# Attention probabilities normalised and masked by GpSimd on copies made by ScalarE, gates in place, PSUM banks six and two

## The chip, the cores and the metric

The kernel runs on one core of one Trainium2 chip. The metric is the device time of one execution in microseconds (us); the time of before is the median of three runs. One further execution was recorded by the hardware profiler; the profile's numbers are of that one. Engines: TensorE (PE; its weight loads are PEld), VectorE (DVE), ScalarE (ACT), GpSimd (POOL), and SyncE (SP), which here only issues DMAs. SBUF is the core's memory of 128 partitions; PSUM is the memory that TensorE writes into, and its eight banks are each one tile of 128 x 512 fp32 here.

## What is computed

Two layers over 1024 tokens and 2048 features. Each layer normalises its input, multiplies it by `w_in`, sends pieces of the result through three heads side by side (sliding-window attention, a gated MLP over chunks, gated linear attention), gates their joint output with silu, and multiplies by `w_out`. Cut to what matters here:

```python
h = rms_norm(x, g_pre) * (1.0 + scale) + shift
a_q, a_k, a_v, s_u, s_v, c_q, c_k, c_v, c_g, z = split(h @ w_in)
# sliding-window attention: blocks of 128 queries, each sees its own block and the one before
scores = einsum('bnqgrd,bnkgd->bngrqk', qb, kb) * 64 ** -0.5
valid = (dist >= 0) & (dist < 128) & (not before the first token)
scores = where(valid, scores, -inf)
m = maximum(scores.max(-1), sink)
p = exp(scores - m)
probs = p / (p.sum(-1) + exp(sink - m))
y_a = einsum('bngrqk,bnkgd->bnqgrd', probs, vb)
y_b = chunked_spatial_gating(gelu(s_u), gelu(s_v), ...)
y_c = rms_norm(gated_linear_attention(c_q, c_k, c_v, log_sigmoid(c_g @ w_up + b) / 16))
out = (concat(y_a, y_b, y_c) * silu(z)) @ w_out
x = x + gate * rms_norm(out, g_post)
```

## The kernel before

**Phases.** Each layer runs over two halves of 512 tokens: four phases, each an `in_phase` (products with `w_in`) and an `out_phase` (products with `w_out`). An `in_phase` goes through groups of output columns; a group fills four PSUM banks from the pool `pj` and adds up over 16 tiles of features. Matrix products are fp32 made of three faster ones (high by high, high by low, low by high): `mm_f` (L382 to L384) for results laid out by feature, `mm_t` (L390 to L392) by token. Every piece of weights is split in high and low by a copy of ScalarE (L368) and a subtraction of VectorE (L369), into a pool of four buffers (`whl`).

**Lanes.** All other work hangs beside the groups: generators in lanes ("att", "gla", "sg", "mod", "fin"). After each three matmuls a group calls `tick()`, and a `yield n` in a lane passes n ticks, that is 3n matmuls of the group. So TensorE's order is a group's triples with the lanes' matmuls between. `drain` runs a lane to its end without ticks; at L810 it does so with the last unit of the first attention call of each phase. A scheduler orders each engine's instructions by priority, and `urgent()` raises it. All PSUM tiles outside the groups come from the pool `mx` (three banks before, `pj` five); who takes one waits until its use before is finished, and TensorE's queue behind it waits too.

**Attention.** There are 32 units, eight in each phase (a pair of heads by four blocks of queries). A unit's scores (L490) go into four `mx` tiles, two at a time; ScalarE copies the previous block's half (L499), VectorE the own block's under a mask (L500), into the tile M. Then come the row maximum, eight exponentials on ScalarE (L516), the sum and its reciprocal, and the product of M with the reciprocal on VectorE (L519, 128 x 1024 elements). After a lag come, for each of the two heads, four transposes on TensorE (L532) and the mask multiplication (L535): VectorE reads the transposed tile from PSUM twice and multiplies by `amask` (k <= q for the own block, k > q for the one before), 128 x 1024 elements into the tile PT. After a further lag the products with the values (L546) follow, which read PT, and a copy on ScalarE (L550). Units 3, 11, 19 and 27 (counted over the kernel) are those that L810 drains.

**Activations.** `silu2` writes tanh into a temporary of the pool t2 (four buffers) and VectorE makes the result from it. `gelu2` copies the bank into a temporary x (L436), squares it into a second, u (L437), and after four more steps the last (L441, on VectorE) reads u and x into the result.

**Gated linear attention (GLA).** `gates` transposes the gate columns (L569) from the tiles that the copy at L767 has brought out of PSUM. `gla_scores` makes its scores at several levels: matmuls `far` (L649) and `near` (L633) into two `mx` tiles, emptied by `put`, VectorE copies under a mask (L620; eight of 32 x 128 after each `near`).

**SyncE** issues all DMAs (weights, inputs, results); GpSimd clears tiles (L496, L598) and masks eight small weights once.

Of the kernel before, what the change touches and what calls it, by code (L numbers as in the profile page):

```python
# [10 lines left out]
F32 = mybir.dt.float32  # L11
# [4 lines left out]
AF = mybir.ActivationFunctionType  # L16
ALU = mybir.AluOpType
AX = mybir.AxisListType
PSUM = bass.MemoryType.PSUM
DRAM = bass.MemoryType.DRAM  # L20

P = 128
# [5 lines left out]
NT = H // P  # L28
# [11 lines left out]
def hybrid_kernel(ctx: ExitStack, tc: tile.TileContext, a, y_out):  # L40
    nc = tc.nc

    const = ctx.enter_context(tc.tile_pool(name="const", bufs=1))
# [5 lines left out]
    sm = ctx.enter_context(tc.tile_pool(name="sm", bufs=2))  # L49
    pj = ctx.enter_context(tc.tile_pool(name="pj", bufs=5, space=PSUM))  # L50
    mx = ctx.enter_context(tc.tile_pool(name="mx", bufs=3, space=PSUM))
    pools = {}

    V, S, G, PE = nc.vector, nc.scalar, nc.gpsimd, nc.tensor

    def load(out, in_):
        nc.sync.dma_start(out=out, in_=in_)
# [38 lines left out]
    def t2(shape=(P, 512), dt=F32):  # L96
        return t2_p.tile(list(shape), dt, tag="t2", name="t2")
# [7 lines left out]
    def mxt():  # L105
        return mx.tile([P, 512], F32, tag="mx", name="mx")

    def pjt():
        return pj.tile([P, 512], F32, tag="pj", name="pj")
# [7 lines left out]
    V.memset(ones, 1.0)  # L117
    amask = const.tile([P, 2, P], F32, name="amask")
    pmask = const.tile([P, P], U8, name="pmask")
# [305 lines left out]
    def silu2(dst, ps):  # L425

        t = t2()
        S.activation(t, ps, AF.Tanh, scale=0.5)
        V.scalar_tensor_tensor(dst, t, 1.0, ps, ALU.add, ALU.mult)

    def gelu2(dst, ps):

        x = t2()
        u = t2()
        with urgent():
            S.copy(x, ps)  # L436
        S.activation(u, x, AF.Square)  # L437
        V.tensor_scalar(u, u, 0.044715, 1.0, ALU.mult, ALU.add)
        V.tensor_tensor(u, u, x, ALU.mult)
        S.activation(u, u, AF.Tanh, scale=GELU_C)  # L440
        V.scalar_tensor_tensor(dst, u, 1.0, x, ALU.add, ALU.mult)  # L441

# [30 lines left out]
    def attention(l, h, g0, qt, vt, cst):  # L473
# [5 lines left out]
        for m in range(4):  # L479
# [3 lines left out]
            for bp in range(2):  # L483
                sps = [mxt().rearrange("p (b k) -> p b k", b=2) for _ in range(2)]
                for b in range(2):
                    n = 2 * bp + b
# [27 lines left out]
            den = col(8, "at_den")  # L514
# [3 lines left out]
            V.reciprocal(den, den)  # L518
            V.tensor_tensor(Mf, Mf, den.unsqueeze(2).broadcast_to([P, 8, P]), ALU.mult)  # L519
            if m < 3:  # L520
# [8 lines left out]
            for p in range(2):  # L529
                tp = mxt()  # L530
                for n in range(NT):
                    PE.transpose(tp[:, n * P:(n + 1) * P], M[:, p, n], ident)  # L532
                pt = pools["pt"].tile([P, 2, NT, P], F32, tag="PT", name="PT")
                with urgent():
                    V.tensor_tensor(pt, tp.rearrange("p (n q) -> p n q", n=NT).unsqueeze(1).broadcast_to([P, 2, NT, P]),  # L535
                                    amask.unsqueeze(2).broadcast_to([P, 2, NT, P]), ALU.mult)
                pts.append(pt)
                yield LAG["t"][p]
# [26 lines left out]

    def gates(l, cg):
        tp = mxt()
        for n in range(NT):
# [445 lines left out]
    with tc.tile_pool(name="start", bufs=1) as st:  # L1014
# [44 lines left out]
        rsqrt(r0, r0, H, st)  # L1059
        psk = [mxt()] + [pjt() for _ in range(5)]  # L1060

# [55 lines left out]
    load(gpc[1], a["g_pre"][1])  # L1117
    load(amask, a["k_amask"])
    pm32 = t2((P, P), I32)
# [33 lines left out]
    for k, (l, h) in enumerate(phases):  # L1153
# [22 lines left out]
        "w_out", "swa_sinks", "sg_w", "sg_b", "sg_ln_g", "sg_ln_b", "gla_w_gate_up", "gla_b_gate", "gla_norm_g",  # L1176
        "k_amask", "k_pmask", "k_gmask", "k_fcol"]


def layout(i):  # L1180
# [48 lines left out]
    k, q = np.meshgrid(r(P), r(P), indexing="ij")  # L1229
    o["k_amask"] = np.stack([k <= q, k > q], axis=1).astype(np.float32)  # L1230
    o["k_pmask"] = (q <= k).astype(np.int32)
# [31 lines left out]
```

## Time and profile before

| | |
|---|---|
| median of three runs | 3062.44 us (3062.06 to 3065.12) |
| the profiled execution | 3067.03 us, its span 3065.3 us |
| mean granted TensorE clock | 0.993 |
| busy: ScalarE, GpSimd | 1229.8 us (40%), 24.5 us (1%) |
| the normalising multiplication, L519 | 32 of 1223 ns |
| the mask multiplication, L535 | 64 of 1221 ns |
| the gelu's copy out of PSUM, L436 | 32 of 576 ns |

Of the profiled execution the page gives each engine's busy time and share, and the chain of work that ended last, followed back from the last instruction. Further views group TensorE's idle time by what ended it (a row says engine, tile and line, "<-", the releaser's engine, tile and line, then the total in us, how often, the longest), give busy times by windows, and list instructions by time. In a row of instructions a bracket at the end is the idle time before it and who ended it. "x8" at a row's end counts instructions that the row gathers.

### The profile page before, as it was taken

The numbers are of one execution on the slowest core, as the hardware profiler recorded it, in microseconds if no ns is written. First come the engines' busy times: TensorE is split into PE (matmuls) and PEld (weight loads), VectorE is DVE, ScalarE is ACT, GpSimd is POOL, SyncE is SP. The second block draws the span as 40 slices with busy tenths as digits, with TensorE's granted clock in tenths as the row PEclk, the third lists the DMA queues.
The fourth block names the chain that finished last, engine by engine and source line by source line (L and its number), as shares of the span: only waits on it lengthen the run. The fifth ranks groups of instructions, "written<-read, shape, count | busy, mean of one in ns | idle before, by whom it ended". The sixth has DMA issues, their size and how long they took to land.

```text
span 3065.3 us, 44211 instructions
## 1 busy us (share of the span) xinstructions
PE 3000.0 (98%) x17298; PEld 2440.8 (80%) x17298; DVE 1840.3 (60%) x2948; ACT 1229.8 (40%) x2415; POOL 24.5 (1%) x66
## 2 busy tenths in 40 slices
PE   8999999999998999999999999999999999999998
PEld 4678777888886888788888788888888888888886
DVE  4668778464767877644364766644346476663425
ACT  3355455232434544323243554423223455442322
POOL 0000000000000000000000000000000000000000
PEclk9999999999999999999999999999999999999999
DMA  9744457475784445544455223334446322343535
GB/s 394 276 138 152 141 179 224 131 243 158 223 255 154 129 138 184 164 126 141 123 159 163 83 73 100 121 114 144 120 124 192 106 83 83 114 133 105 165 103 162
DMA packets 214914, 468.98 MB, mean 153 GB/s; under 512 B 21008, under 2 KB 72624, under 8 KB 212656
## 3 DMA queue, kind: packets, MB, share of 16 engines
q1 hardware_dynamic: 214704, 466.15, 48.6%
q8 instruction: 136, 2.23, 0.3%
q14 instruction: 74, 0.61, 0.1%
HBM read 429.37 MB, written 36.70 MB: 152 GB/s over the span
## 4 chain that ended last, share of the span: by engine, by line
PE 81%; DVE 8%; DMA 6%; ACT 3%; issue 2%; SPq 0%; DVEq 0%; ACTq 0%
PE pj L382 12%; PE pj L390 12%; PE pj L392 12%; PE pj L383 12%; PE pj L384 12%; PE pj L391 12%; DMA wm<-in_w_mod_dram 3%; PE mx L490 2%; PE mx L546 2%; DVE whl L369 2%; DVE ma L225 1%; PE mx L532 1%; ACT whl L368 1%; PE mx L1076 1%; DMA t<-in_x_dram 1%
## 5 line engine op out<-in xcount | busy, mean ns | idle before, releaser
L369 DVE TENSOR_TENSOR whl<-wraw,whl 128x1024 fp32r<-128x1024 f32 (+2 forms) x504 | 587.3, 1166 | 720.9 <-ACT whl L368 719.9
L368 ACT CAST whl<-wraw 128x1024 fp32r<-128x1024 f32 (+2 forms) x504 | 505.0, 1002 | 1048.3 <-PE pj L392 494.6
L390 PE MATMUL pj<-whl,act 128*128 128x512 f32 (+1 forms) x2048 | 785.0, 383 | 0.5 <-ACT hold L767 0.5
L392 PE MATMUL pj<-whl,act 128*128 128x512 f32 (+1 forms) x2048 | 778.5, 380 | 0.0
L391 PE MATMUL pj<-whl,act 128*128 128x512 f32 (+1 forms) x2048 | 775.9, 379 | 0.0
L382 PE MATMUL pj<-act,whl 128*128 128x512 f32 x1904 | 756.4, 397 | 9.1 <-ACT t L436 8.2
L383 PE MATMUL pj<-act,whl 128*128 128x512 f32 x1904 | 744.2, 391 | 0.0
L384 PE MATMUL pj<-act,whl 128*128 128x512 f32 x1904 | 742.6, 390 | 0.0
L392 PEld LDWEIGHTS pj<-whl,act 128*128 128x128 f32 x2048 | 385.6, 188 | 72.2 <-issue 0.3
L390 PEld LDWEIGHTS pj<-whl,act 128*128 128x128 f32 x2048 | 386.3, 189 | 70.8 <-issue 2.5
L391 PEld LDWEIGHTS pj<-whl,act 128*128 128x128 f32 x2048 | 386.0, 188 | 67.0 <-issue 0.8
L382 PEld LDWEIGHTS pj<-act,whl 128*128 128x128 f32 x1904 | 358.5, 188 | 100.4 <-issue 14.3
L384 PEld LDWEIGHTS pj<-act,whl 128*128 128x128 f32 x1904 | 358.6, 188 | 76.5
L383 PEld LDWEIGHTS pj<-act,whl 128*128 128x128 f32 x1904 | 358.9, 188 | 70.7 <-issue 0.7
L225 DVE SCALAR_TENSOR_TENSOR ma<-wm,sc,ma 128x512 f32<-128x512 f32 x240 | 179.9, 750 | 61.6 <-DMA wm<-in_w_mod_dram 58.7
L516 ACT ACTIVATE M<-M,at_nm 128x128 f32<-128x128 f32 x256 | 99.6, 390 | 19.4 <-DVE at_nm L508 19.4
L535 DVE TENSOR_TENSOR PT<-mx,amask 128x1024 f32<-128x1024 f32 x64 | 77.8, 1221 | 17.1 <-PE mx L532 17.0
L500 DVE COPY_PREDICATED M<-pmask,mx 128x256 f32<-128x256 uint8 x128 | 51.2, 442 | 53.5 <-ACT M L499 41.5
L490 PE MATMUL mx<-kc,qs 128*128 128x256 f32 (+1 forms) x256 | 66.2, 288 | 10.5 <-DVE hold L620 5.9
L490 PE MATMUL mx<-kc,qlo 128*128 128x256 f32 (+1 forms) x256 | 65.8, 285 | 0.0
L499 ACT COPY M<-mx 128x256 f32<-128x256 f32 x96 | 31.7, 375 | 80.7 <-PE mx L490 80.7
L490 PEld LDWEIGHTS mx<-kc,qs 128*128 128x128 f32 x256 | 49.3, 193 | 17.7 <-issue 7.1
(230 smaller groups left out, 2390.1 us busy)
## 6 DMA issues: line engine op xcount, KB each, us to landing
wraw<-in_w_in_dram SPq DMA_DIRECT2D x312, 512.0 KB, 3.6
wraw<-in_w_out_dram SPq DMA_DIRECT2D x136, 512.0 KB, 3.6
wm<-in_w_mod_dram SPq DMA_DIRECT2D x256, 256.0 KB, 3.7
wm<-in_w_mod_dram SPq DMA_DIRECT2D x16, 2048.0 KB, 13.7
y<-at SPq DMA_DIRECT2D x64, 256.0 KB, 2.9
q<-y SPq DMA_DIRECT2D x64, 256.0 KB, 2.8
q<-x SPq DMA_DIRECT2D x36, 256.0 KB, 2.7
wraw<-in_w_vcg_dram SPq DMA_DIRECT2D x32, 272.0 KB, 2.8
```

The lines of the kernel that those rows point to most:

```text
L225: V.scalar_tensor_tensor(acc, ws[k], sc[:, k:k + 1], acc, ALU.mult, ALU.add)
L368: S.copy(hl[:, 0], raw)
L369: V.tensor_tensor(hl[:, 1], raw, hl[:, 0].bitcast(F32), ALU.subtract)
L382: PE.matmul(ps, lhsT=whi, rhs=slot[:, 0], start=(k == 0), stop=False)
L383: PE.matmul(ps, lhsT=whi, rhs=slot[:, 1], start=False, stop=False)
L384: PE.matmul(ps, lhsT=wlo, rhs=slot[:, 0], start=False, stop=(k == NK - 1))
L390: PE.matmul(ps, lhsT=slot[:, 0, c], rhs=whi, start=(k == 0), stop=False)
L391: PE.matmul(ps, lhsT=slot[:, 0, c], rhs=wlo, start=False, stop=False)
L392: PE.matmul(ps, lhsT=slot[:, 1, c], rhs=whi, start=False, stop=(k == NK - 1))
L490: PE.matmul(sps[p][:, b, k0:], lhsT=qi[:, p, n * P:(n + 1) * P], rhs=kc[2 * j + p][:, n * P + k0:n * P + 256], start=(part == 0), stop=(pa ...
L516: S.activation(Mf[:, k], Mf[:, k], AF.Exp, bias=nm[:, k:k + 1], scale=0.125, accum_out=den[:, k:k + 1])
L535: V.tensor_tensor(pt, tp.rearrange("p (n q) -> p n q", n=NT).unsqueeze(1).broadcast_to([P, 2, NT, P]), amask.unsqueeze(2).broadcast_to([P, ...
```

## The change

- The product of M with the reciprocals (L519) runs on GpSimd instead of VectorE.
- The mask multiplication (L535) is replaced: for each head two ScalarE copies of 128 x 512 from PSUM into PT's halves, then two GpSimd selects that put zero where the mask is zero. The constant `amask` and its load go.
- `silu2` and `gelu2` work in place: silu needs no temporary, gelu copies PSUM into the result's own tile (`hold`) and needs one.
- `gates` passes five ticks ahead of its transposes.
- `pj` has six banks and `mx` two, instead of five and three; the first group of the program takes all its six from `pj`.

```diff
-    pj = ctx.enter_context(tc.tile_pool(name="pj", bufs=5, space=PSUM))
-    mx = ctx.enter_context(tc.tile_pool(name="mx", bufs=3, space=PSUM))
+    pj = ctx.enter_context(tc.tile_pool(name="pj", bufs=6, space=PSUM))
+    mx = ctx.enter_context(tc.tile_pool(name="mx", bufs=2, space=PSUM))
...
     def silu2(dst, ps):
 
-        t = t2()
-        S.activation(t, ps, AF.Tanh, scale=0.5)
-        V.scalar_tensor_tensor(dst, t, 1.0, ps, ALU.add, ALU.mult)
-
-    def gelu2(dst, ps):
-
-        x = t2()
-        u = t2()
+        S.activation(dst, ps, AF.Tanh, scale=0.5)
+        V.scalar_tensor_tensor(dst, dst, 1.0, ps, ALU.add, ALU.mult)
+
+    def gelu2(x, ps):
+
         with urgent():
             S.copy(x, ps)
+        u = t2()
         S.activation(u, x, AF.Square)
         V.tensor_scalar(u, u, 0.044715, 1.0, ALU.mult, ALU.add)
         V.tensor_tensor(u, u, x, ALU.mult)
         S.activation(u, u, AF.Tanh, scale=GELU_C)
-        V.scalar_tensor_tensor(dst, u, 1.0, x, ALU.add, ALU.mult)
+        V.scalar_tensor_tensor(x, u, 1.0, x, ALU.add, ALU.mult)
...
-            V.tensor_tensor(Mf, Mf, den.unsqueeze(2).broadcast_to([P, 8, P]), ALU.mult)
+            G.tensor_tensor(Mf, Mf, den.unsqueeze(2).broadcast_to([P, 8, P]), ALU.mult)
...
                 with urgent():
-                    V.tensor_tensor(pt, tp.rearrange("p (n q) -> p n q", n=NT).unsqueeze(1).broadcast_to([P, 2, NT, P]),
-                                    amask.unsqueeze(2).broadcast_to([P, 2, NT, P]), ALU.mult)
+                    for w in range(2):
+                        S.copy(pt[:, w], tp.rearrange("p (n q) -> p n q", n=NT))
+
+                    G.affine_select(pt[:, 0], pt[:, 0], pattern=[[0, NT], [1, P]], compare_op=ALU.is_ge, fill=0.0, base=0,
+                                    channel_multiplier=-1)
+                    G.affine_select(pt[:, 1], pt[:, 1], pattern=[[0, NT], [-1, P]], compare_op=ALU.is_gt, fill=0.0, base=0,
+                                    channel_multiplier=1)
...
     def gates(l, cg):
+        yield 5
         tp = mxt()
...
-        psk = [mxt()] + [pjt() for _ in range(5)]
+        psk = [pjt() for _ in range(6)]
```

Lines move by up to a dozen: L382 to L384 become L381 to L383, L390 to L392 become L389 to L391, L436 becomes L432, L490 L487, L532 L529, L546 L548, L633 L636.

What the scheduler makes of it is shown at three places. In these rows stands a line, an operation, the tile that it writes, "<-", the tiles that it reads, and the shape.

ScalarE, at the first gelu group of the first phase, with the engines whose semaphores each instruction waits for. Before, the last two of the group's four copies, and what stands about them (L264 and L513, L516 are other lanes' work):

```order
L436 COPY t2_4225<-pj_3717 128x512 [waits DVE_49]
L264 ACTIVATE junk_4658,xss_4506<-wm_4654 128x128 [waits Activation_49]
L437 ACTIVATE t2_4226<-t2_4225 128x512 [waits Activation_49]
L264 ACTIVATE junk_4660,xss_4506<-wm_4654 128x128 [waits Activation_49]
L440 ACTIVATE t2_4217<-t2_4217 128x512 [waits DVE_49]
L264 ACTIVATE junk_4662,xss_4506<-wm_4654 128x128 [waits Activation_49]
L368 CAST whl_4376<-wraw_4249 128x1024 [waits DMAHW3_49,PE_49]
L264 ACTIVATE junk_4723,xss_4506<-wm_4721 128x128 [waits DMAHW2_49,Activation_49]
L436 COPY t2_4234<-pj_3718 128x512 [waits DVE_49]
```

The same place after:

```order
L432 COPY hold_4242<-pj_3739 128x512 [waits PE_49]
L432 COPY hold_4250<-pj_3740 128x512 [waits PE_49]
L513 ACTIVATE M_4136,at_den_4206<-M_4136,at_nm_4201 128x128
L432 COPY hold_4258<-pj_3741 128x512 [waits PE_49]
L432 COPY hold_4266<-pj_3742 128x512 [waits PE_49]
L367 CAST whl_4360<-wraw_4194 128x1024 [waits DMAHW7_49]
L434 ACTIVATE t2_4244<-hold_4242 128x512 [waits Activation_49]
L434 ACTIVATE t2_4252<-hold_4250 128x512 [waits Activation_49]
```

The third and fourth copies no longer wait for VectorE; all four stand together and wait for TensorE alone.

TensorE, at the drained unit 11 in the second phase. Before (M is the unit's probabilities, PT_9850 and PT_9857 its two heads after transposing and masking, v the values; L233 is another lane's):

```order
L532 MATMUL mx_9845<-ident_81,M_9746 128x128 x4
L532 MATMUL mx_9852<-ident_81,M_9746 128x128 x4
L391 MATMUL pj_9889<-whl_9734,act_6768 128x512
L392 MATMUL pj_9889<-whl_9734,act_6768 128x512
L390 MATMUL pj_9890<-whl_9734,act_6768 128x512
L391 MATMUL pj_9890<-whl_9734,act_6768 128x512
L392 MATMUL pj_9890<-whl_9734,act_6768 128x512
L390 MATMUL pj_9887<-whl_9734,act_6789 128x512
L391 MATMUL pj_9887<-whl_9734,act_6789 128x512
L392 MATMUL pj_9887<-whl_9734,act_6789 128x512
L546 MATMUL mx_9859<-PT_9850,v_8015 64x128
```

After:

```order
L529 MATMUL mx_9885<-ident_81,M_9734 128x128 x4
L529 MATMUL mx_9895<-ident_81,M_9734 128x128 x4
L389 MATMUL pj_9935<-whl_9723,act_6790 128x512
L390 MATMUL pj_9935<-whl_9723,act_6790 128x512
L391 MATMUL pj_9935<-whl_9723,act_6790 128x512
L389 MATMUL pj_9936<-whl_9723,act_6790 128x512
L548 MATMUL mx_9905<-PT_9890,v_8037 64x128
L390 MATMUL pj_9936<-whl_9723,act_6790 128x512
L391 MATMUL pj_9936<-whl_9723,act_6790 128x512
L389 MATMUL pj_9933<-whl_9723,act_6811 128x512
L548 MATMUL mx_9905<-PT_9900,v_8037 64x128
```

Between the transposes and the first product with the values stood eight matmuls of the group, and now four; the second head's first product comes three further on.

TensorE, in the third phase, where GLA's `near` (the rows of x32) meets the next unit's scores (kc are keys, qs and qlo queries). Before:

```order
L633 MATMUL mx<-hold 32x32 x32
L390 MATMUL pj<-whl,act 128x512
L391 MATMUL pj<-whl,act 128x512
L392 MATMUL pj<-whl,act 128x512
L490 MATMUL mx<-kc_1087,qs 128x128
L490 MATMUL mx<-kc_1087,qlo 128x128
L490 MATMUL mx<-kc_1087,qs 128x256
L490 MATMUL mx<-kc_1087,qlo 128x256
L390 MATMUL pj<-whl,act 128x512
L391 MATMUL pj<-whl,act 128x512
L392 MATMUL pj<-whl,act 128x512
L490 MATMUL mx<-kc_1088,qs 128x128
```

After:

```order
L487 MATMUL mx<-kc_1085,qs 128x256
L487 MATMUL mx<-kc_1085,qlo 128x256
L487 MATMUL mx<-kc_1086,qs 128x256
L487 MATMUL mx<-kc_1086,qlo 128x256
L389 MATMUL pj<-whl,act 128x512
L390 MATMUL pj<-whl,act 128x512
L391 MATMUL pj<-whl,act 128x512
L389 MATMUL pj<-whl,act 128x512
L636 MATMUL mx<-hold 32x32 x32
L390 MATMUL pj<-whl,act 128x512
L391 MATMUL pj<-whl,act 128x512
L389 MATMUL pj<-whl,act 128x512
```

The scores stood three and six matmuls behind `near`; now the unit's last scores stand four matmuls ahead of it, and only the group's triples follow.

More of the change, by code (lines that the diff above doesn't have):

```diff
@@ L117, in hybrid_kernel @@
     V.memset(ones, 1.0)
-    amask = const.tile([P, 2, P], F32, name="amask")
     pmask = const.tile([P, P], U8, name="pmask")
@@ L1117, in hybrid_kernel @@
     load(gpc[1], a["g_pre"][1])
-    load(amask, a["k_amask"])
     pm32 = t2((P, P), I32)
@@ L1176 @@
         "w_out", "swa_sinks", "sg_w", "sg_b", "sg_ln_g", "sg_ln_b", "gla_w_gate_up", "gla_b_gate", "gla_norm_g",
-        "k_amask", "k_pmask", "k_gmask", "k_fcol"]
+        "k_pmask", "k_gmask", "k_fcol"]
 def layout(i):
@@ L1229, in layout @@
     k, q = np.meshgrid(r(P), r(P), indexing="ij")
-    o["k_amask"] = np.stack([k <= q, k > q], axis=1).astype(np.float32)
     o["k_pmask"] = (q <= k).astype(np.int32)
```

## Prediction

> **What bounds the kernel now.** I read the page's table of engines and chain of waits first, then TensorE's own waits, grouped by who ended them.
>
> ```profile
> PE 3000.0 (98%) x17298; PEld 2440.8 (80%) x17298; DVE 1840.3 (60%) x2948; ACT 1229.8 (40%) x2415; POOL 24.5 (1%) x66
> ...
> PE 81%; DVE 8%; DMA 6%; ACT 3%; issue 2%; SPq 0%; DVEq 0%; ACTq 0%
> ```
> ```profile
> PE mx L1056 <- DVE s L1055: 8.3, 1, 8.3
> PE pj L382 <- ACT t L436: 8.2, 6, 3.5
> PE mx L1076 <- DMA wm<-in_w_mod_dram: 6.9, 4, 2.1
> PE mx L490 <- DVE hold L620: 5.9, 5, 2.3
> PE mx L569 <- ACT v L767: 5.5, 2, 3.0
> ...
> PE mx L532 <- DVE M L519: 3.1, 2, 2.7
> PE mx L490 <- ACT qs L470: 2.8, 2, 2.5
> ```
> TensorE is busy for 98% of the span and carries 81% of the chain. The change alters none of its matmuls, so it can win or lose only where TensorE stands still or runs slowly. The second fence has, for each pair, the total wait in us, how often, and the longest. The start-up rows (L1056, L1076) are out of the change's reach. A wait also has a price after it, which the view by windows shows (busy times of PE, PEld, DVE, ACT, POOL, then granted clock):
>
> ```profile
> 164.30:167.70 3.40, 3.40 (x9) 2.63 (x9) 2.76 (x4) 1.52 (x2) 0.00 (x0) 0.50 0.91 294
> 512.90:516.30 3.40, 3.30 (x9) 2.64 (x10) 3.35 (x7) 1.85 (x5) 0.00 (x0) 0.56 0.73 230
> 922.10:925.50 3.40, 3.40 (x10) 2.42 (x11) 0.96 (x2) 1.93 (x4) 0.00 (x0) 0.50 0.87 295
> 993.70:997.20 3.50, 3.50 (x14) 3.11 (x13) 1.13 (x3) 1.26 (x3) 0.00 (x0) 0.51 0.02 5
> ```
> These follow the two L569 waits, the longest L436 wait and the longest L620 wait (2.3 to 3.5 us each). For 3.4 us the clock stands at about half: (1 - 0.50) x 3.4 = 1.7 us of work lost. So a wait of over about 2.3 us costs 1.7 us more than its row says.
>
> **The change part by part.** The sum is made against the profiled execution, 3067.0 us; the median of the runs is 3062.4, so I carry the difference over to the median.
>
> *Gelu in place.* L436's copies free the banks for the next group, but they wait:
> ```profile
>   DVE hold L441: 9.1, 8
> ```
> That is who ended ScalarE's idle time ahead of L436: the copies need a t2 tile, whose last reader is L441 on VectorE. After the change the copy goes straight into its hold tile, and in the order ScalarE's four copies wait for TensorE alone. So 8.2 goes, and 0.44 x 3.4 = 1.5 of the window at 512.9: **-9.7**. What is late next is the copy itself, once the group's last matmul is done; with six banks for groups of four, two are free meanwhile.
>
> *Gates.* Five ticks of three matmuls now stand ahead of the transposes at L569. Fifteen matmuls spaced 0.23 us (1110.01 to 1110.24, below) are 3.4 us, more than the longest wait of 3.0. So 5.5 goes, with two windows of 1.7: **-8.9**.
>
> *Scores behind GLA's puts.* The scores (L490) took a bank that eight small DVE copies (L620) had to empty first:
> ```profile
> 990.39 2.03 DVE L620 COPY_PREDICATED hold<-gmask,mx 32x128 f32<-32x128 uint8 x8
> ```
> In the new order the scores come first and GLA's matmuls behind them (the rows at the change), and what next wants a bank stands over thirty matmuls later. So 5.9 goes, with the window at 993.7 (0.49 x 3.5 = 1.7): **-7.6**. Elsewhere some small ones come back, counted with the banks.
>
> *Normalising on GpSimd.* Two rows give the price: what the step takes now, and the only kind of GpSimd work on data of this size in the trace, alone and beside VectorE:
> ```profile
> L519 DVE TENSOR_TENSOR M<-M,at_den 128x1024 f32<-128x1024 f32 x32 | 39.1, 1223 | 0.8
> ```
> ```profile
> 1284.68 0.64 POOL L880 TENSOR_SCALAR_AFFINE_SELECT hold<-hold 128x512 f32<-128x512 f32 x1 [54.69 <-DMA hold<-in_sg_w_dram]
> 1289.29 1.54 POOL L880 TENSOR_SCALAR_AFFINE_SELECT hold<-hold 128x512 f32<-128x512 f32 x1 [3.98 <-DMA hold<-in_sg_w_dram]
> ```
> ```profile
> 1289.12 1.22 DVE L369 TENSOR_TENSOR whl<-wraw,whl 128x1024 fp32r<-128x1024 f32 x1
> ```
> One input of 512 takes 0.64, so 1024 with two inputs is estimated at 4 x 0.64 = 2.5 us; the lower end is VectorE's 1.22, the upper 4 x 1.54 = 6.2, if all of it ran as the select beside L369 did. I take 2.5, because most selects would meet no such operation for their whole length. The page "GPSIMD Engine Reference" of the Trainium skill (§ 3.1 Elementwise) speaks against this part: it gives GpSimd 4497 ns where VectorE needs 2293, for 2048 elements of fp32. Halved to 1024 that is an estimate of 2.25 us, and three drained units would each wait 0.3 us less by it.
>
> Most units have room, four have none. An ordinary unit and the drained unit 11, first DVE, then PE:
> ```profile
> 1162.07 1.22 DVE L519 TENSOR_TENSOR M<-M,at_den 128x1024 f32<-128x1024 f32 x1
> ```
> ```profile
> 1164.05 0.27 PE L532 MATMUL mx<-ident,M 128*128 128x128 f32 x1
> ```
> ```profile
> 1107.50 1.22 DVE L519 TENSOR_TENSOR M<-M,at_den 128x1024 f32<-128x1024 f32 x1
> ...
> 1110.11 2.35 DVE L535 TENSOR_TENSOR PT<-mx,amask 128x1024 f32<-128x1024 f32 x2
> ```
> ```profile
> 1108.87 1.06 PE L532 MATMUL mx<-ident,M 128*128 128x128 f32 x8
> 1109.69 0.48 PE L391 MATMUL pj<-whl,act 128*128 128x512 f32 x1
> 1110.01 0.40 PE L392 MATMUL pj<-whl,act 128*128 128x512 f32 x1
> 1110.24 0.40 PE L390 MATMUL pj<-whl,act 128*128 128x512 f32 x1
> ...
> 1111.72 0.43 PE L546 MATMUL mx<-PT,v 128*64 128x128 f32 x2
> ```
> The ordinary unit's transposes start 0.76 us after L519's end (1163.29); unit 11's start 0.15 after it, straight upon it. 2.5 instead of 1.22 makes unit 11's transposes 1.3 us late, and its sisters 19 and 27, at the same place of their phases: 3 x 1.3 = **+4**. Unit 3, the first phase's sister, waits 2.7 already (the L519 row); its new order keeps four more us of matmuls between scores and transposes than the other three have, so I leave it. By the same two views four more units (1, 4, 12 and 15) start within 0.15 of L519's end, and nine have 0.7 to 1.4 us of room; in the new order most of these get 0.3 to 1.5 us more matmuls ahead, unit 12 gets 0.9 fewer. For them **+2**. What queues behind the slow operation on GpSimd is only the next unit's memset and the masks; behind the waiting transposes, all of TensorE.
>
> *Masking on GpSimd.* Instead of one operation of 1.22 us per half
> ```profile
> L535 DVE TENSOR_TENSOR PT<-mx,amask 128x1024 f32<-128x1024 f32 x64 | 77.8, 1221 | 17.1 <-PE mx L532 17.0
> ```
> come two copies and two selects, on two engines in turn. The nearest copy is
> ```profile
> L436 ACT COPY t<-pj 128x512 f32<-128x512 f32 x32 | 18.4, 576 | 17.8 <-DVE hold L441 9.1 <-PE pj L384 8.5
> ```
> In a drained unit both halves arrive together: one copy, then four selects in a row, 0.58 + 4 x 0.64 = 3.1 us from the end of the first half's transposes, some 2.6 from the end of the second's. The order now puts seven matmuls (1.6 us) before the first use of the second half, where eight stood. That is 1.0 late, and half as much for a cast of ScalarE that may lie ahead of the copies: 1.5 x 4 = **+6**. The ends are 0 (every copy prompt) and 0.58 + 4 x 1.54 = 6.7, so 4.6 late, or 18. Ordinary units have twenty matmuls and more between (4.5 us). Two of these eight waits should pass 2.3 us or come close together: two windows, **+3.4**.
>
> *Two banks instead of three for all but the groups.* Who takes a bank now waits for the use two back, not three. A pair of banks with scores is emptied like this (PE, ACT, DVE):
> ```profile
> 1099.44 0.28 PE L490 MATMUL mx<-kc,qlo 128*128 128x256 f32 x1
> ```
> ```profile
> 1099.52 0.65 ACT L499 COPY M<-mx 128x256 f32<-128x256 f32 x2 [2.37 <-PE mx L490]
> ```
> ```profile
> 1099.92 0.78 DVE L500 COPY_PREDICATED M<-pmask,mx 128x256 f32<-128x256 uint8 x2 [2.24 <-ACT M L499]
> ```
> That is 1.2 us from the last matmul's start. I count fourteen places in the order where only about four to nine matmuls stand between (GLA's matmuls behind scores, PV behind a put, scores behind PV). The ends are 0 and 14 x 1.1 = 15; I take 0.4 each, **+6**, nearer the lower end because the matmuls between cover most of it.
>
> *Switches.* A matmul of a group after one of another kind is spaced 0.32 (1109.69 to 1110.01) instead of 0.23. The order has 356 changes between the two kinds instead of 381: 25 x 0.09 = **-2**.
>
> *Load off VectorE.* The two removed operations are 77.8 + 39.1 = 117 us. VectorE isn't the bound, but the queries' chain (L470's input) runs through it: that row's 2.8 with one window, 4.5, may go or stay; I take half, **-2**.
>
> Sum: -9.7 - 8.9 - 7.6 + 4 + 2 + 6 + 3.4 + 6 - 2 - 2 = -8.8. That is 3058.2 for the profiled execution and **3053.6 by the median; I say 3054**. ScalarE's 128 new copies, 128 x 0.58 = 74 us, lie in the 60% of its time that is idle, and the casts of the weights, which they may delay, have four buffers ahead of TensorE; where that cover is missing, a copy costs up to 0.58.
>
> **The rivals.**
>
> *Slower: GpSimd is held by VectorE.* The select at 1289.29 ended 0.49 us after L369 had ended (1290.34) and took 1.54 for 0.64; so VectorE's two-input operations may hold GpSimd off. If the normalising takes 2.5 + 1.22 = 3.7, units with about 1 us of room wait as well. Then the three drained units lose 1.2 more each, the nine with 0.7 to 1.4 of room about 1 each, the four drained masks 1 more each, with five windows of 1.7 in place of two: 3.6 + 9 + 4 + 5 = +22 on the forecast, or 3076. It decides once the operation takes more than about 3.2 us in most units. For it: that row. Against it: VectorE is at 60% and will be lower, and L369 is short. Chance 0.20. The page "SBUF — State Buffer" (§ Who interferes with whom) of the Trainium skill has this as a rule: a VectorE instruction with two SBUF inputs and a GpSimd instruction that reads SBUF shut each other out for a whole instruction. The trace agrees in that one direction, by the 0.49.
>
> *No change: half-clock windows and banks eat it.* Every one of the four drained units gets two windows (8 x 1.7 = 14 in place of 3.4), or the banks cost 15 in place of 6: 10 more, about 3064. For it: the rows show 1.7 us for a wait of 2.3. Chance 0.14.
>
> *The waits only move.* The copies of L436 are let go but stand behind another ScalarE operation, and the gates' transposes wait for something else: if half of the two wins comes back, (9.7 + 8.9) / 2 = 9, about 3063. Against it: the order names no other releaser there. Chance 0.08.
>
> *Better: VectorE's relief counts.* The other half of L470's 4.5 and unit 3's wait with what follows it (2.7 + 1.7) go too, and half of the banks' 6 and of the masks' 9.4 is covered: 3054 - 2 - 4.4 - 3 - 4.7 = 3040. For it: L519's late units are those where VectorE was behind. Against it: GpSimd is the slower engine for the same chain. Chance 0.12.
>
> **How the numbers follow.** The forecast's own case has 0.46. About 0.2% (6 us) is what a measurement of this kernel can tell from no change: faster is under 3056.3, slower over 3068.6. Faster: 0.40 of the forecast's case, 0.12 and 0.02, 0.54. Same: 0.06 + 0.13 + 0.06 + 0.02 = 0.27. Slower: 0.18 + 0.01 = 0.19. The range reaches from just under the better case to the lower part of the slower one, 3037 to 3075.
>
> **What would show it.** Right: no row of TensorE waiting for the gelu copy or for the gates' input, GLA's puts nearly gone as a releaser of scores, and new waits of 1 to 3 us at units 11, 19 and 27 for a POOL operation of about 2.5 us. Wrong: POOL's normalising at over 3.2 us and waits of transposes in more than ten units (the slower rival); a mean granted clock under 0.99 (windows); many waits of scores or PV on banks (two banks too few).

## The result, and the profile after

The changed kernel is slower: a median of 3072.75 us (19 runs, 3067.86 to 3080.16) against 3065.12 us for the kernel before on the same chips (19 runs). The ratio is 1.0023, with a 95% interval of 1.0016 to 1.0030: some 7 us lost, where 9 won were forecast. The profiled execution took 3070.68 us with a span of 3068.7, against 3067.03 and 3065.3, so the records show 3.7 us of it.

The table of engines of the changed kernel:

```profile
PE 3000.3 (98%) x17298; PEld 2439.6 (80%) x17298; DVE 1781.8 (58%) x2852; ACT 1290.9 (42%) x2543; POOL 198.5 (6%) x226
```

VectorE had 77.8 + 39.1 = 117 us of work taken off its 1840.3. It should stand at 1723 and stands at 1781.8: 58 us came back in some other form. What TensorE waits for now (total, times, longest):

```profile
PE mx L529 <- POOL M L516: 12.6, 8, 3.4
...
PE mx L487 <- DVE M L497: 4.5, 3, 2.8
PE pj L381 <- ACT v L770: 4.3, 2, 3.2
...
PE mx L561 <- DVE M L497: 2.8, 2, 2.5
...
PE mx L548 <- POOL PT L535: 2.4, 4, 0.7
PE mx L548 <- DVE hold L623: 2.0, 1, 2.0
PE mx L487 <- ACT qs L467: 1.8, 2, 1.5
PE mx L548 <- POOL PT L537: 0.9, 3, 0.4
PE mx L529 <- DVE hold L623: 0.9, 1, 0.9
```

The gelu's copy (8.2 before) and the puts as releaser of scores (5.9) are gone, as forecast. In their place stand the normalised tile from GpSimd (12.6, where the row of VectorE had 3.1), the copies of v, now waited for by the next group in place of the transposes, and waits for banks (L497, L623).

GpSimd's groups after, with their mean lengths in ns:

```profile
L516 POOL TENSOR_TENSOR M<-M,at_den 128x1024 f32<-128x1024 f32 x32 | 64.4, 2013 | 724.5 <-DVE at_den L515 331.0 <-ACT hold L697 195.5 <-ACT q L770 60.1
L537 POOL TENSOR_SCALAR_AFFINE_SELECT PT<-PT 128x512 f32<-128x512 f32 x64 | 58.5, 914 | 0.0
L535 POOL TENSOR_SCALAR_AFFINE_SELECT PT<-PT 128x512 f32<-128x512 f32 x64 | 56.9, 889 | 148.2 <-ACT PT L533 148.1
```

The product is quicker than the estimated 2.5 us: 1.9 in most units, 2.0 on average. A single product is thus only 0.7 us longer than on VectorE. Something else that it does is seen where the longest wait is, first GpSimd's and then VectorE's instructions by time (start, length):

```profile
1225.05 2.12 POOL L516 TENSOR_TENSOR M<-M,at_den 128x1024 f32<-128x1024 f32 x1 [24.49 <-ACT t L434]
```
```profile
1224.98 0.43 DVE L435 TENSOR_SCALAR t<-t 128x512 f32<-128x512 f32 x1
1225.45 2.27 DVE L436 TENSOR_TENSOR t<-t,hold 128x512 f32<-128x512 f32 x1
1227.64 0.75 DVE L435 TENSOR_SCALAR t<-t 128x512 f32<-128x512 f32 x2
```

L436's multiplication of 128 x 512 took 2.27 us, and ended 0.55 us after GpSimd's product did (1227.17). The same operation took 0.687 before (L439 there). VectorE was held in it until GpSimd's product was over. Of the kernel before, L439, and L611, which is L614 after:

```profile
L439 DVE TENSOR_TENSOR t<-t,t 128x512 f32<-128x512 f32 x32 | 22.0, 687 | 0.5
...
L611 DVE TENSOR_TENSOR hold<-hold 128x256 f32<-128x256 f32 x40 | 16.9, 422 | 0.2
```

The place at 241 us shows both directions:

```profile
238.27 2.82 POOL L516 TENSOR_TENSOR M<-M,at_den 128x1024 f32<-128x1024 f32 x1 [35.07 <-DVE at_den L515]
```
```profile
238.66 0.68 DVE L609 TENSOR_TENSOR hold<-hold 128x512 f32<-128x512 f32 x1
239.38 2.00 DVE L614 TENSOR_TENSOR hold<-hold 128x256 f32<-128x256 f32 x1
```
```profile
241.15 0.66 PE L529 MATMUL mx<-ident,M 128*128 128x128 f32 x4 [2.11 <-POOL M L516]
```

GpSimd's product overlaps VectorE's two-input operations and takes 2.82 instead of 1.90; then L614, 0.42 long before, takes 2.00. TensorE's transposes wait 2.11 us, in an ordinary unit that L810 does not drain. Not all of that wait is GpSimd's: with the product and the masks back on VectorE (e4 below) the same unit still waits 1.39 us.

### The profile page after: what moved, and what is told of

It is laid out like the page before. It is cut to its first block, busy times and chain, and to the rows that moved or that the text cites. A ratio compares the mean times of both kernels' runs of the same rounds, so it can differ in the third digit from the quotient of the medians.

```text
span 3068.7 us, 44482 instructions
## 1 busy us (share of the span) xinstructions
PE 3000.3 (98%) x17298; PEld 2439.6 (80%) x17298; DVE 1781.8 (58%) x2852; ACT 1290.9 (42%) x2543; POOL 198.5 (6%) x226
## 4 chain that ended last, share of the span: by engine, by line
PE 82%; DVE 7%; DMA 5%; ACT 3%; issue 2%; POOL 1%; SPq 0%; DVEq 0%; ACTq 0%; POOLq 0%
PE pj L381 13%; PE pj L382 13%; PE pj L383 12%; PE pj L389 12%; PE pj L391 12%; PE pj L390 12%; DMA wm<-in_w_mod_dram 3%; PE mx L487 2%; PE mx L548 2%; DVE ma L224 2%; DVE whl L368 1%; PE mx L529 1%; PE mx L1079 1%; ACT whl L367 1%; DMA q<-in_x_f_dram 1%
## 5 line engine op out<-in xcount | busy, mean ns | idle before, releaser
L368 DVE TENSOR_TENSOR whl<-wraw,whl 128x1024 fp32r<-128x1024 f32 (+2 forms) x504 | 596.8, 1185 | 759.9 <-ACT whl L367 756.9
L389 PE MATMUL pj<-whl,act 128*128 128x512 f32 (+1 forms) x2048 | 783.3, 382 | 0.0
L391 PE MATMUL pj<-whl,act 128*128 128x512 f32 (+1 forms) x2048 | 777.9, 380 | 0.0
L390 PE MATMUL pj<-whl,act 128*128 128x512 f32 (+1 forms) x2048 | 775.9, 379 | 0.0
L381 PE MATMUL pj<-act,whl 128*128 128x512 f32 x1920 | 761.6, 397 | 7.3 <-ACT v L770 4.3
L382 PE MATMUL pj<-act,whl 128*128 128x512 f32 x1920 | 749.3, 390 | 0.0
L383 PE MATMUL pj<-act,whl 128*128 128x512 f32 x1920 | 747.8, 390 | 0.0
L381 PEld LDWEIGHTS pj<-act,whl 128*128 128x128 f32 x1920 | 361.0, 188 | 107.1 <-issue 22.4
L391 PEld LDWEIGHTS pj<-whl,act 128*128 128x128 f32 x2048 | 385.4, 188 | 71.9 <-issue 0.2
L389 PEld LDWEIGHTS pj<-whl,act 128*128 128x128 f32 x2048 | 385.8, 188 | 68.6 <-issue 2.6
L390 PEld LDWEIGHTS pj<-whl,act 128*128 128x128 f32 x2048 | 385.8, 188 | 68.1 <-issue 1.3
L383 PEld LDWEIGHTS pj<-act,whl 128*128 128x128 f32 x1920 | 360.9, 188 | 76.6 <-issue 0.3
L382 PEld LDWEIGHTS pj<-act,whl 128*128 128x128 f32 x1920 | 361.3, 188 | 71.8 <-issue 0.7
L224 DVE SCALAR_TENSOR_TENSOR ma<-wm,sc,ma 128x512 f32<-128x512 f32 x240 | 184.7, 770 | 63.5 <-DMA wm<-in_w_mod_dram 60.7
L513 ACT ACTIVATE M<-M,at_nm 128x128 f32<-128x128 f32 x256 | 99.6, 391 | 32.2 <-DVE at_nm L505 32.2
L516 POOL TENSOR_TENSOR M<-M,at_den 128x1024 f32<-128x1024 f32 x32 | 64.4, 2013 | 724.5 <-DVE at_den L515 331.0
L601 POOL MEMSET hold<- 128x512 f32 x16 | 8.3, 526 | 1384.3 <-DMA wraw<-in_w_ck_dram 664.4
L533 ACT COPY PT<-mx 128x512 f32<-128x512 f32 x128 | 68.0, 589 | 44.7 <-PE mx L529 41.4
L497 DVE COPY_PREDICATED M<-pmask,mx 128x256 f32<-128x256 uint8 x128 | 50.7, 440 | 47.4 <-ACT M L496 36.3
L487 PE MATMUL mx<-kc,qs 128*128 128x256 f32 (+1 forms) x256 | 67.1, 292 | 7.0 <-DVE M L497 4.5
L548 PEld LDWEIGHTS mx<-PT,v 128*64 128x64 f32 x960 | 54.0, 140 | 20.5 <-issue 12.7
## 6 DMA issues: line engine op xcount, KB each, us to landing
wm<-in_w_mod_dram SPq DMA_DIRECT2D x16, 2048.0 KB, 13.4
```

What stands on the lines that cost most here:

```text
L224: V.scalar_tensor_tensor(acc, ws[k], sc[:, k:k + 1], acc, ALU.mult, ALU.add)
L368: V.tensor_tensor(hl[:, 1], raw, hl[:, 0].bitcast(F32), ALU.subtract)
L381: PE.matmul(ps, lhsT=whi, rhs=slot[:, 0], start=(k == 0), stop=False)
L382: PE.matmul(ps, lhsT=whi, rhs=slot[:, 1], start=False, stop=False)
L383: PE.matmul(ps, lhsT=wlo, rhs=slot[:, 0], start=False, stop=(k == NK - 1))
L389: PE.matmul(ps, lhsT=slot[:, 0, c], rhs=whi, start=(k == 0), stop=False)
```

## The experiments

All are timed against the kernel before on the same chip; "ratio" is that of the times, with its 95% interval. 0.001 is 3.07 us.

| run | ratio to before | interval |
|---|---|---|
| the changed kernel | 1.0023 | 1.0016 to 1.0030 |
| e1_norm_vector | 0.9989 | 0.9980 to 0.9998 |
| e2_mask_vector | 1.0004 | 0.9992 to 1.0015 |
| e3_banks_five_three | 1.0029 | 1.0019 to 1.0039 |
| e4_all_vector | 0.9948 | 0.9933 to 0.9963 |
| e5_dummy_on_gpsimd | 0.9991 | 0.9982 to 1.0001 |
| e6_late_by_scalar | 0.9939 | 0.9925 to 0.9952 |
| e7_inplace_yield_53 | 0.9936 | 0.9924 to 0.9948 |
| e8_inplace_alone | 0.9961 | 0.9948 to 0.9975 |
| e9_dummy_memsets | 0.9946 | 0.9933 to 0.9959 |
| e10_dummy_selects | 0.9974 | 0.9964 to 0.9984 |
| e11_norm_gpsimd_alone | 1.0054 | 1.0040 to 1.0067 |

### Undoing one part of the change

**e1**, the normalising back on VectorE:

```diff
-            G.tensor_tensor(Mf, Mf, den.unsqueeze(2).broadcast_to([P, 8, P]), ALU.mult)
+            V.tensor_tensor(Mf, Mf, den.unsqueeze(2).broadcast_to([P, 8, P]), ALU.mult)
```


> The changed kernel with one thing undone: the normalising multiplication is back on VectorE, all else (masks on GpSimd, gates, in place, banks six and two) as changed. Theory A (GpSimd's slower, later product holds TensorE): the changed kernel's 8 waits of transposes for it, 12.6 us, and the half-speed window at 1226 (3.4 us) go, about 3 us of such waits stay; 10 to 13 us less than the changed kernel, that is 0.998 to 0.999 of the kernel before. Rival B (two banks are what costs): the waits for L516 go but waits on banks take their place; within 4 us of the changed kernel, ratio to before 1.001 to 1.002.

**e2**, the masks back on VectorE (its one multiplication by `amask` per head, as before; the normalising stays on GpSimd):

```diff
-                    for w in range(2):
-                        S.copy(pt[:, w], tp.rearrange("p (n q) -> p n q", n=NT))
...
-                    G.affine_select(pt[:, 0], ...)
-                    G.affine_select(pt[:, 1], ...)
+                    V.tensor_tensor(pt, tp..., amask..., ALU.mult)
```


> The changed kernel with the masking undone alone: VectorE multiplies by the mask out of PSUM as before, the normalising stays on GpSimd. Theory A: of the 46 us by which VectorE's two-input operations grew, only those that fall on the 32 products are left (under 25); the waits of the values' products for POOL (2.4 and 0.9) go; the waits for the product on GpSimd stay at 8 to 13 us; 3 to 6 us less than the changed kernel. If instead the masks on GpSimd are a help (they take 78 us off VectorE), it is 0 to 5 us slower than the changed kernel. Rival B: no change, within 2 us.

**e3**, banks five and three:

```diff
-    pj = ctx.enter_context(tc.tile_pool(name="pj", bufs=6, space=PSUM))
-    mx = ctx.enter_context(tc.tile_pool(name="mx", bufs=2, space=PSUM))
+    pj = ctx.enter_context(tc.tile_pool(name="pj", bufs=5, space=PSUM))
+    mx = ctx.enter_context(tc.tile_pool(name="mx", bufs=3, space=PSUM))
...
-        psk = [pjt() for _ in range(6)]
+        psk = [mxt()] + [pjt() for _ in range(5)]
```


> The changed kernel with banks five and three as before, all else as changed. Theory B (two banks cost): the waits for banks in the changed kernel (L487 and L561 for L497 4.5 and 2.8, L548 and L529 for L623 2.0 and 0.9: 10.2 us, with three half-speed windows of 1.7) go and some 3 to 6 us of scores waiting for L623 come back: 7 to 12 us less than the changed kernel, ratio to before 0.998 to 1.000. Theory A: those waits go likewise but the 12.6 us for the product on GpSimd stay, and with one bank fewer the gates' copies (4.3) hold the next group longer: within 4 us of the changed kernel.

**e4**, e1 and e2 together: only gelu and silu in place, the five ticks and the banks are left of the change.

> The changed kernel with normalising and masking both back on VectorE; gates, in place and banks six and two as changed. If GpSimd's part (theory A) is the loss: VectorE's two-input operations are back at their lengths of before, the waits for POOL go, and 10 to 16 us less than the changed kernel, ratio to before 0.997 to 0.999. If the banks (B) are the loss, it stays above the kernel before: ratio 1.001 to 1.003, with waits for L497 and L623 of 8 us and more.

The normalising on VectorE gives 10 us (1.0023 to 0.9989), the masks 6 (to 1.0004), both together 23 (to 0.9948). That is more than 10 and 6 added, and more than the 10 to 16 expected of e4; why the two don't add up is not shown. The banks give nothing (1.0029), and e3 waits for the product on GpSimd as the changed kernel does:

```profile
PE mx L529 <- POOL M L516: 12.5, 8, 2.7
...
PE mx L487 <- DVE M L497: 7.7, 6, 2.2
```

Theory B, that two banks cost the time, falls: with a bank more the time is no lower, and the scores even wait longer for their copies (7.7 against 4.5). The loss is GpSimd's part. VectorE's total agrees: 1794.3 us in e1 and 1829.4 in e2 by their pages, where 1840.3 less the work taken off would be 1762.5 and 1801.2; the masks bring back 31.8 and the product 28.2, together 60, near the changed kernel's 58.

How much TensorE waits for the normalised tile, in e2 and then in e4:

```profile
PE mx L530 <- POOL M L517: 14.7, 8, 2.9
```
```profile
PE mx L530 <- DVE M L517: 7.3, 5, 2.4
```

So five units wait for it with VectorE too, in the new order (in e1 three, 3.4 us), and the 12.6 us of the changed kernel are not all GpSimd's. From e4 to e2 the wait grows by 7.4 us, from e1 to the changed kernel by 9.2. TensorE stands still 13.4 us longer in e2 than in e4 in all (by the pages, span less TensorE's busy time: 69.2 against 55.8); the other 6 are waits for other results. These rows don't tell whether the tile is late because the product is longer on GpSimd or because the two engines hold each other up.

### Late tile or held VectorE?

Both explain why the product on GpSimd costs. **e5** puts contention without lateness of GpSimd's result: the kernel of e4 with a useless product on GpSimd. It works on constants and the reciprocals, writes a tile of bf16, and nobody reads its result.

```diff
             V.tensor_tensor(Mf, Mf, den.unsqueeze(2).broadcast_to([P, 8, P]), ALU.mult)
+            G.tensor_tensor(gjunk, ident.unsqueeze(1).broadcast_to([P, 8, P]), den.unsqueeze(2).broadcast_to([P, 8, P]), ALU.mult)
```


> The kernel of e4_all_vector plus one useless product on GpSimd in each of the 32 units, of the size of the normalising one (128 x 1024, two inputs in SBUF), started when the reciprocals are ready; nobody waits for its result, and the order of TensorE, VectorE and ScalarE is the same instruction for instruction. Theory C (GpSimd's operations hold VectorE's two-input operations, whatever they compute): some of VectorE's operations stretch to 2 us and more, in all by 15 to 30 us, and the time is 4 to 10 us over e4, ratio to before 0.996 to 0.998. Theory L (only the lateness of the normalised tile counts): no change against e4, ratio to before 0.994 to 0.996.

**e6** was to put lateness without contention:

```diff
             V.tensor_tensor(Mf, Mf, den.unsqueeze(2).broadcast_to([P, 8, P]), ALU.mult)
+            S.copy(Mf[:, 0:4], Mf[:, 0:4])
```


> The kernel of e4_all_vector, and behind the normalising product on VectorE a copy of half the tile onto itself on ScalarE (128 x 512, about 0.6 us), for which the transposes wait: the tile is 0.7 us later, as with GpSimd's 1.9 us in place of 1.22, and GpSimd does nothing more. Theory L: the waits of the transposes grow by 3 to 6 us, with a window more or two, the time is 4 to 9 us over e4. Theory C: under 3 us over e4.

e5 is 13 us slower than e4 (0.9991), beyond what was expected; e6 is no slower at all (0.9939), though its copy took 620 ns in each unit. But e6 does not settle what lateness costs. The scheduler made another order for it, different from e4's at some sixty places on TensorE, and in that order TensorE's waits for the tile did not even grow from e4's 7.3 us:

```profile
PE mx L531 <- ACT M L518: 5.6, 5, 1.9
```

The drained units 11, 19 and 27, which wait 1.0 us each in the changed kernel, do not wait in e6. So a lateness of 0.6 us can be hidden by the order; its price in e4's own order was not tried.

TensorE, VectorE and ScalarE ran the same instructions in the same order in e4 and e5. The table of engines of e4, then of e5, and e5's groups on VectorE and, last, GpSimd's product:

```profile
PE 2996.1 (98%) x17298; PEld 2440.0 (80%) x17298; DVE 1841.3 (60%) x2948; ACT 1230.4 (40%) x2415; POOL 26.6 (1%) x66
```
```profile
PE 2992.1 (98%) x17298; PEld 2436.0 (80%) x17298; DVE 1869.0 (61%) x2948; ACT 1227.2 (40%) x2415; POOL 117.8 (4%) x98
...
L535 DVE TENSOR_TENSOR PT<-mx,amask 128x1024 f32<-128x1024 f32 x64 | 77.5, 1218 | 13.0 <-PE mx L532 12.6
L518 DVE TENSOR_TENSOR M<-M,at_den 128x1024 f32<-128x1024 f32 x32 | 45.9, 1436 | 0.9
```
```profile
L519 POOL TENSOR_TENSOR gjunk<-ident,at_den 128x1024 bf16<-128x1024 f32 x32 | 91.4, 2855 | 857.6 <-DVE at_den L517 495.5 <-ACT hold L695 219.4 <-ACT hold L434 44.9
```

27.7 us more on VectorE for the same 2948 instructions, as much as the real product brings in e2 (28.2), although the useless one is longer (2.86 us on average against 2.01). L518, with two inputs in SBUF, grew from 1223 to 1436 ns on average: four of the 32 were held to 2.92. L535, with one of its two in PSUM, kept its 1218. So a product that nobody waits for costs 13 us, by holding VectorE; that is most of the 17 that the product costs from e4 to e2. Some lateness is in these 13 as well, since the four held L518 finish their tiles 1.7 us late, and whether the other 4 us are GpSimd's late tile is not shown: the intervals are too wide. The recorded execution of e5 was the shortest of its twelve (3058.2 us against a median of 3064.7), so its trace shows less than the median lost: its waits for L518 are 9.2 us where e4 has 7.3, for L535 2.9 where e4 has none.

### Which work on GpSimd holds?

**e9** and **e10** put other useless work on GpSimd into e4, again without touching any other engine's order: four memsets at the place of the product, or the 128 selects behind the masks, into a tile that nobody reads.

```diff
+            G.tensor_copy(gjunk[:, 0:8], den)
+            for _ in range(4):
+                G.memset(gjunk, 0.0)
```


> The kernel of e4_all_vector plus, in each of the 32 units, a copy of 128 x 8 and four memsets of 128 x 512 on GpSimd (4 x 0.53 us), started when the reciprocals are ready; nobody waits for them, and the order of TensorE, VectorE and ScalarE is the same instruction for instruction. If GpSimd holds VectorE only where it reads SBUF, VectorE's lengths stay as in e4 (no operation of 2 us), ratio to before 0.994 to 0.996. If any GpSimd work of 2 us at that place holds it, VectorE grows by 15 us and more as in e5 and the ratio is 0.998 to 1.000.

```diff
+                for w in range(2):
+                    G.affine_select(gjunk.rearrange("p (n q) -> p n q", n=NT), pt[:, w], ...)
```


> The kernel of e4_all_vector plus the changed kernel's 128 selects of 128 x 512 on GpSimd, which here read the masked tile and write into a tile that nobody reads; the order of TensorE, VectorE and ScalarE is the same instruction for instruction. Theory C: VectorE's two-input operations grow by 15 to 30 us and the time by 6 to 12 us over e4, about what the masks cost in e1_norm_vector: ratio to before 0.997 to 0.999. If in e1 it was the lateness of the masks and the 128 copies on ScalarE that cost, it is within 3 us of e4: 0.994 to 0.996.

Of e9, the table of engines and GpSimd's two new groups; then the same of e10:

```profile
PE 2989.3 (98%) x17298; PEld 2434.9 (80%) x17298; DVE 1843.1 (61%) x2948; ACT 1228.0 (40%) x2415; POOL 132.0 (4%) x226
...
L521 POOL MEMSET gjunk<- 128x512 f32 x128 | 68.4, 535 | 7.3
L519 POOL COPY gjunk<-at_den 128x8 f32<-128x8 f32 x32 | 36.8, 1151 | 837.9 <-DVE at_den L517 504.5 <-ACT hold L697 216.8 <-ACT hold L434 43.0
```
```profile
PE 2999.8 (98%) x17298; PEld 2442.2 (80%) x17298; DVE 1861.9 (61%) x2948; ACT 1228.9 (40%) x2415; POOL 143.8 (5%) x194
...
L537 POOL TENSOR_SCALAR_AFFINE_SELECT gjunk<-PT 128x512 f32<-128x512 f32 x128 | 118.7, 927 | 851.0 <-DVE PT L534 844.0 <-DVE el L685 2.0
```

68 us of memsets leave VectorE at its 1841 (1843.1) and the time at e4's (0.9946). The selects, which read SBUF, add 20.6 us to VectorE and 8 us to the time (0.9974): two thirds of what the masks cost in e1 against e4 (12.6). What holds VectorE's two-input operations is GpSimd's reading, not the time spent there. e9's copy of eight elements per partition, 1.15 us on average, shows the other direction. One of them, and VectorE's product at that time:

```profile
1143.93 1.15 POOL L519 COPY gjunk<-at_den 128x8 f32<-128x8 f32 x1 [21.82 <-DVE at_den L517]
```
```profile
1143.81 1.22 DVE L518 TENSOR_TENSOR M<-M,at_den 128x1024 f32<-128x1024 f32 x1
```

It ends 0.05 us after the product. The page "SBUF — State Buffer" of the Trainium skill (§ Who interferes with whom) says that a VectorE instruction with two SBUF inputs contends with a GpSimd instruction that reads SBUF, not with one that only writes it; e5, e9 and e10 agree with it.

### One part alone

**e11**, the kernel before with only the product on GpSimd (the diff is e1's, turned round).

> The kernel before with one thing changed: the normalising product on GpSimd. Theory C, by the difference of e2_mask_vector and e4_all_vector (17 us) and by e5_dummy_on_gpsimd (13 us): slower than before by 10 to 18 us, ratio 1.003 to 1.006. By the prediction's terms for it (+4, +2 and a window or two): 1.002 to 1.003.

**e8**, the kernel before with only gelu and silu in place, and **e7**, that with the five ticks as well; everything on VectorE, banks five and three.

> The kernel before with gelu and silu in place alone. By the prediction's first term the waits for the gelu's copy (8.2) and the window behind the longest (1.5 to 1.7) go, and nothing else: 8 to 11 us less than before, ratio 0.9963 to 0.9975. If the waits for the copies only turn into waits for banks or weights, within 3 us of before.

> The kernel before with gelu and silu in place and the five ticks in the gates, banks five and three, normalising and masks on VectorE: e4_all_vector with the banks put back. If six and two banks are worth something beside the in-place step, it is slower than e4 by 3 to 8 us (the gates' copies hold the group longer, over 4 us of waits for L766; scores wait for L619), ratio to before 0.996 to 0.998; if two banks cost, it is faster than e4, ratio 0.991 to 0.994.

e11 loses 16.6 us (1.0054). Of its waits, the first two:

```profile
PE pj L382 <- ACT t L436: 10.9, 8, 4.3
PE mx L532 <- POOL M L519: 9.8, 7, 3.2
```

Its span is 16.6 us longer than that of before, too (3081.9 against 3065.3). Of that TensorE stands still 12.9 and is busy 3.7 longer. The tile's row grew by 6.7 (from 3.1), which is near the +4 and +2 of the prediction; the other 6.2 are waits for other results, such as the gelu's copies (8.2 before), whose temporaries VectorE has to free.

e8 wins 12 (0.9961), e7 20 (0.9936): the lowest ratio of the table, ahead of the kernel before and of the changed one, though its interval overlaps those of e4, e6 and e9. e8 and e7 tell the gates' term from the puts' term. Of e8, then of e7, in TensorE's waits:

```profile
PE mx L488 <- DVE hold L618: 6.0, 5, 2.3
PE mx L567 <- ACT v L765: 4.8, 2, 3.0
```
```profile
PE mx L530 <- DVE M L517: 5.5, 4, 1.8
PE pj L382 <- ACT v L766: 5.1, 2, 2.7
```

The five ticks take away the scores' wait for the puts (6.0), with the banks as they were. They don't take away the wait for v (4.8, then 5.1). ScalarE's record of the changed kernel tells why, with TensorE's first matmul after it:

```profile
922.89 1.04 ACT L367 CAST whl<-wraw 128x1024 fp32r<-128x1024 f32 x1 [3.13 <-DVE ma L224]
923.84 1.24 ACT L770 COPY v<-pj 128x272 f32<-128x272 f32 x4
```
```profile
924.27 0.50 PE L381 MATMUL pj<-act,whl 128*128 128x512 f32 x1 [3.23 <-ACT v L770]
```

ScalarE stood idle for 3.13 us in front of a cast, with the copies of v queued behind it. The releaser named there (L224) works on other data; in the kernel before and in e7 the cast at the same place waits for its weights' DMA:

```profile
920.35 1.04 ACT L368 CAST whl<-wraw 128x1024 fp32r<-128x1024 f32 x1 [2.95 <-DMA wraw<-in_w_in_dram]
```
```profile
910.63 1.05 ACT L368 CAST whl<-wraw 128x1024 fp32r<-128x1024 f32 x1 [2.73 <-DMA wraw<-in_w_in_dram]
911.58 1.24 ACT L766 COPY v<-pj 128x272 f32<-128x272 f32 x4
```

The copies are late whoever asks for them. With the transposes moved away, the next group's third bank asks.

## Why the prediction was wrong

- **Gelu in place** (-9.7): right. e8 wins 12.0 us (8 to 16 by its interval), and of the 8.2 us of waits for the copy 0.2 are left in its record.
- **Gates** (-8.9): failed. "More than the longest wait" only held for the transposes; the copies were as late as before and the next group waits for them, 4.3 us instead of 5.5. That the two free banks cover this, as I had said for the gelu, does not hold for groups whose copies stand behind a cast that waits for a DMA. The two windows behind the waits are missing in the changed kernel's record (the one behind 3.23 us too), but they are there in e7's at 164 and 911.
- **Scores behind the puts** (-7.6): right, by e8's row, which e7's record no longer has; it was the five ticks that did it, not the banks.
- **Normalising on GpSimd** (+4, +2 and part of the windows): this is the step that failed. I priced the tile's lateness alone, and put what the product does to VectorE's own operations at nothing. The operation's length was even overestimated, and the lateness was about as forecast: at the drained units three waits of 1.0 us at 1105, 1852 and 2589 against three of 1.3, in e11 6.7 us more in all (9.8 against 3.1) against 6. But the cost is 16.6 us in e11 and 17 from e4 to e2, VectorE's operations grew by 28.2 us in e2 and 26.5 in e11, and e5 shows 13 us of cost with nobody waiting for GpSimd. "**Load off VectorE**" (-2) failed with it: 117 us of work went and 58 us of standing still came.
- **Masking on GpSimd** (+6 and +3.4 of windows): the size is near (12.6 from e4 to e1, 6 from e2 to the changed kernel), the mechanism for the most part not: the waits for PT are 3.3 us, and the selects alone, with nobody waiting for them, cost 8.
- **Two banks** (+6): not contradicted, but not shown either: e7, with three banks, is 3.7 us faster than e4, as was expected of it if two banks cost, but the intervals overlap, and with GpSimd at work e3 shows no gain from a third bank. Which bank waits are GpSimd's doing stays open.
- **Switches** (-2) were not tried by themselves.

The sum of the terms outside GpSimd was -22; e4 has -15.9 (-20.5 to -11.3); its record still shows 3.6 us of waits for v, and 4.2 more than before for the normalised tile. GpSimd's terms were +13 and are +23. Two errors with one sign turned -9 into +7.

The measured 3072.75 lies inside the range of 3037 to 3075, and that is luck: it lies at the end that another mechanism, GpSimd held by VectorE, had been given. Of the named signs of being wrong two did not appear (eight units wait and not more than ten, for a product of 2.0 us and not over 3.2; the clock is 0.993 and not under 0.99), and the third, many waits on banks, is open to reading (seven, 10.2 us). No sign looked at the lengths of VectorE's operations, where the loss stood.

The slower rival had the right pair of engines and a fifth of the chance. Its condition was wrong: it should have decided "once the operation takes more than about 3.2 us", and the product takes 1.9, its longest 2.82. I had read the row of 1.54 us as GpSimd being held by VectorE, which it is, and left out the other direction, though the page "SBUF — State Buffer" of the Trainium skill (§ Who interferes with whom), cited there, has both. In the trace of before GpSimd had so little to do that no operation of VectorE grew.

## What to carry to other kernels

Moving an operation to an idle engine can cost more by what it does to the engine it leaves than by its own length: here 64 us of products on GpSimd brought VectorE 28 us of standing still and the kernel 17 us, though GpSimd was busy for only 3% of the time and VectorE for 60% (e2). A test that tells lateness from contention is cheap: add the operation as useless work that nobody waits for, and add the lateness on a third engine. The second half is worth something only if the order stays the same, which in e6 it did not. And a wait is removed only if its releaser gets earlier; if only the one who waits is moved, look for who asks next (the next bank here).

## What was not expected of the hardware

- VectorE's copies under a mask and its reductions never grew beside GpSimd (L497: 440 ns against 442 before), nor did the product with one input in PSUM (1218 ns); the two-input operations in SBUF did, up to 2.9 us. So did some operations with one input: in the changed kernel a TENSOR_SCALAR (L222, 0.48 us before) reached 2.12 beside the product, and in e9 seven (L437, 0.42 undisturbed) took 0.70 to 0.83 beside the memsets, which only write.
- The product of 128 x 1024 took 1.9 us on GpSimd, as long as three selects of 128 x 512 (0.63 each undisturbed), and not four as I had reckoned.
- The half-speed windows don't follow the length of a wait strictly. In the changed kernel 3.23 us at 924 and 2.30 at 353 have none, as these windows show (clock in the third column from the end), while the wait of 2.0 at 1049 does:

```profile
924.00:927.40 3.40, 3.12 (x15) 2.47 (x16) 1.20 (x1) 1.91 (x5) 0.00 (x0) 1.00 0.86 277
353.00:356.40 3.40, 2.92 (x16) 2.18 (x17) 3.37 (x5) 2.05 (x4) 2.13 (x5) 1.00 0.37 78
1049.00:1052.40 3.40, 3.40 (x32) 3.18 (x32) 1.87 (x3) 0.00 (x0) 0.00 (x0) 0.52 0.57 182
```
